# Storing the delta rule's solved blocks straight from where they are solved

## The chip, the cores and the metric

The kernel runs on one core of one Trainium2 chip. The metric is the device time of one execution in microseconds (us); lower is better. The engines are TensorE (PE, with its weight loads PEld), VectorE (DVE), ScalarE (ACT), GpSimd (POOL) and SyncE (SP), which issues nearly all transfers; a few are issued by ScalarE's own queue. 16 DMA engines carry the transfers.

## The reference, cut to what matters

The model has two layers over 512 latent tokens and 256 context tokens, width 1024: a bidirectional gated DeltaNet, then attention. The change lies in the DeltaNet layer, in the matrix that the chunked delta rule needs for each chunk of 64 tokens, each of 16 value heads and both directions:

```
a = jnp.where(strict, jnp.einsum('bhncd,bhnsd->bhncs', kb, kc) * decay, 0.0)
eye = jnp.eye(DN_CHUNK, dtype=F32)
t_inv = lax.linalg.triangular_solve(eye + a, jnp.broadcast_to(eye, a.shape),
                                    left_side=True, lower=True, unit_diagonal=True)
u = jnp.einsum('bhncs,bhnse->bhnce', t_inv, vb)
w = jnp.einsum('bhncs,bhnsd->bhncd', t_inv, kb * jnp.exp(gc)[..., None])
```

`t_inv` is a lower triangular 64x64 matrix per chunk, head and direction. Split in 32x32 blocks it has two solved blocks on the diagonal, one block beside it that is a product of the two and of the block of `a` between them, and one block that is zero. The recurrence reads it as the operand `cT`.

## The kernel before, in words

All is in fp32; the large products are split in a high and a low half (`wh`, `wl`, `uh`, `ul`) and made of three matmuls each. The first stage normalises the inputs and computes the modulation. The second, which the change touches (from about 100 to 602 us), projects the heads one after the other: eight key heads, eight query heads (`q_head`, numbered 0 to 7 here), then 16 value heads (`v_head`) and 16 gate heads (`z_head`) mixed. A head is 48 matmuls into PSUM tiles `g` (four buffers; a head uses two, so head n + 2 reuses those of head n), a convolution over tokens (L357 a copy by ScalarE, L360 four steps of VectorE per half) and a gate (L363 tanh by ScalarE, L372 for query heads and L365 for value heads by VectorE, into `sil_q`, `sil_v`). Its weights come three heads ahead: load L318 on SP, cast L319 on ScalarE, low half L320 on POOL or VectorE.

Between the heads run the pieces of the delta rule's matrices, for six tiles t of 128 rows (two chunks each) with 16 heads in the free dimension:
- `t_masked`: the keys' products are masked (`Gx`, L604, L605) and the decay between tokens is made. Its rows `df` are loaded on SP (L573), turned by ScalarE into exp(-|difference|) (L579, 16 activations of 128x64, then L580), and multiplied by VectorE (L560) into `md` (the diagonal blocks) and `mo` (the blocks beside it). L624 transposes `md` on VectorE into `L`, L625 scales it on POOL.
- `t_solve`: for two tiles at a time 31 steps of two instructions on POOL (L679, L680), from `L` to `X`.
- `t_join`: L695 turns `X` into `U0` and `U1` on VectorE, PE multiplies `mo` with one of them (`pp`), ScalarE negates it (`pn`, L707), PE multiplies again (`pw`, L713). ScalarE gathers the solved blocks from `U` (L705, eight copies of 32x512 a tile) and the products from PSUM (L716, four copies) in `Tt`, whose other blocks L555 has set to zero once on POOL, and L717 stores `Tt` to `t_d` in DRAM in one transfer of 1 MB. There are two `Tt`.
- `t_queries`: the decayed products of queries and keys (`df0q`, `df1q`, `qk_d`), on PE, VectorE, ScalarE and POOL.

`pieces` gives the order of these: the masks of tiles 0 and 1, then the solve of a pair woven with the masks of the next, then the joins of tiles 0 and 1 and the queries woven with the third solve, then the joins of tiles 2 to 5. After each head one to three pieces are written. That written order goes to a builder which orders each engine's instructions by its own estimates of their times; an engine then runs its instructions strictly in that order. Transfers on SP go out in its order too, each after the one eight before it has landed.

In the third stage, from 602 us, the recurrence reads `t_d` back as `cT` (L953); its first matmuls are L990.

Of the kernel before, what the change touches and what calls it, by code (L numbers as in the profile page):

```python
# [8 lines left out]
F32 = mybir.dt.float32  # L9
# [8 lines left out]
P = 128  # L18
# [4 lines left out]
NT = 6  # L23
QH, VH = 8, 16
# [73 lines left out]
def backbone(tc, a, out):  # L98
    nc = tc.nc
    V, S, G, T = nc.vector, nc.scalar, nc.gpsimd, nc.tensor  # L100
    dma = nc.sync.dma_start
# [8 lines left out]
    def dtile(shape, name):  # L110
        return dram.tile(shape, F32, tag=name, name=name)
# [15 lines left out]
    t_d = dtile([NT, P, 2, VH, 64], "t_d")  # L127
# [328 lines left out]
    for v in range(2):  # L456
        for d in range(2):
            c0 = ((v ^ d) * 2 + d) * 96
# [84 lines left out]

    tpool = tc.tile_pool(name="tpool", bufs=1, side="right", reuse_waits="tile")
    tp = tpool.__enter__()
    Tts = [tp.tile([P, 2, VH, 64], F32, tag=f"Tt{i}", name=f"Tt{i}") for i in range(2)]

    def of(b, d):

        return d ^ (b // 2)  # L550

    for Tt in Tts:
        for b in range(4):
            c0 = 32 - (b % 2) * 32
            G.memset(Tt[b * 32:b * 32 + 32, of(b, 1 - b % 2), :, c0:c0 + 32], 0.0)  # L555

    def decayed(E, o, dec, x):

# [128 lines left out]
    def t_join(t, st_):  # L687

        nm = f"_{t}"
        X, mo = st_[t - t % 2][1][:, t % 2], st_["mo", t]  # L690
        Tt = Tts[t % 2]

        U = [tp.tile([P, 2, VH, 32], F32, tag=f"U{d}", name=f"U{d}" + nm) for d in range(2)]
        for d, z_ in enumerate((X, X.rearrange("p i j -> p j i"))):
            V.transpose(U[d].rearrange("p v h j -> p j (v h)"), z_)  # L695
        yield
        pp = pa.tile([P, VH, 32], F32, tag="gq", name="pp" + nm)
        for h in range(VH):
            for b in range(4):
                i0, o0, d = b * 32, (b ^ 1) * 32, 1 - b % 2  # L700
                T.matmul(pp[o0:o0 + 32, h, :], mo[i0:i0 + 32, h, :], U[d][i0:i0 + 32, of(b, d), h, :], start=True, stop=True, tile_position=(i0, o0))
        for b in range(4):
            for d in range(2):
                r, c0 = slice(b * 32, b * 32 + 32), (b % 2) * 32
                S.copy(Tt[r, of(b, d), :, c0:c0 + 32], U[d][r, of(b, d)])  # L705
        pn = tp.tile([P, VH, 32], F32, tag="pn", name="pn" + nm)
        S.activation(pn, pp, AF.Copy, scale=-1.0)  # L707
        yield
        pw = pa.tile([P, VH, 32], F32, tag="gq", name="pw" + nm)
        for h in range(VH):  # L710
            for b in range(4):
                i0 = b * 32
                T.matmul(pw[i0:i0 + 32, h, :], U[1 - b % 2][i0:i0 + 32, of(b, b % 2), h, :], pn[i0:i0 + 32, h, :], start=True, stop=True, tile_position=(i0, i0))  # L713
        for b in range(4):
            c0 = 32 - (b % 2) * 32
            S.copy(Tt[b * 32:b * 32 + 32, of(b, b % 2), :, c0:c0 + 32], pw[b * 32:b * 32 + 32])  # L716
        dma(t_d[t], Tt)  # L717
        yield

    def side_by_side(*gens):  # L720
# [24 lines left out]
    def pieces():  # L745

        st_ = {}
        masked = lambda a, b: t_masked((a, b), st_)
        join = lambda a, b: one_by_one(t_join(a, st_), t_join(b, st_))
        queries = t_queries()  # L750
        yield from masked(0, 1)
        yield from weave(t_solve(0, st_), masked(2, 3), 2)
        yield from weave(t_solve(2, st_), masked(4, 5), 2)
        yield from weave(t_solve(4, st_), one_by_one(join(0, 1), queries), 3)
        yield from join(2, 3)
        yield from join(4, 5)
# [822 lines left out]
    po = pS.tile([P, 512], F32, tag="po", name="po1")  # L1579
# [49 lines left out]
    with tc.tile_pool(name="fo", bufs=2, side="right", reuse_waits="tile") as f2, tc.tile_pool(name="psO", bufs=1, space=PSUM, reuse_waits="tile") as pO:  # L1629
# [9 lines left out]
        for t in range(4):  # L1639
# [6 lines left out]
            for nh in range(2):  # L1646
                c = slice(nh * 512, nh * 512 + 512)
# [7 lines left out]
            r = ss[:, t, 0:1]  # L1655
# [3 lines left out]
            for hf in range(2):  # L1659
                c = t if hf == 0 else 7 - t  # L1660
# [35 lines left out]
```

## Time and profile before

| | us |
|---|---|
| three runs, median (lowest, highest) | 1264.22 (1263.83, 1269.48) |
| the profiled execution | 1262.34 |
| its span in the trace | 1260.6 |
| PE, DVE, ACT, POOL busy | 1155.4, 846.0, 714.9, 601.0 |

The span runs from the first to the last instruction that the profile shows; 1.7 us of the profiled execution's time lie outside it. Busy time of PE includes time at a lower granted clock. In the views, `out<-in` names the tiles an instruction writes and reads, `x48` is the count, and what stands in brackets behind a row of the timeline is the engine's idle time before it and what ended it.

### The profile page before, as it was taken

The numbers are of one execution on the slowest core, as the hardware profiler recorded it, in microseconds if no ns is written. First come the engines' busy times: TensorE is split into PE (matmuls) and PEld (weight loads), VectorE is DVE, ScalarE is ACT, GpSimd is POOL, SyncE is SP. The second block draws the span as 40 slices with busy tenths as digits, with TensorE's granted clock in tenths as the row PEclk, the third lists the DMA queues.
The fourth block names the chain that finished last, engine by engine and source line by source line (L and its number), as shares of the span: only waits on it lengthen the run. The fifth ranks groups of instructions, "written<-read, shape, count | busy, mean of one in ns | idle before, by whom it ended". The sixth has DMA issues, their size and how long they took to land.

```text
span 1260.6 us, 28128 instructions
## 1 busy us (share of the span) xinstructions
PE 1155.4 (92%) x10755; PEld 927.4 (74%) x10755; DVE 846.0 (67%) x1895; ACT 714.9 (57%) x1923; POOL 601.0 (48%) x486
## 2 busy tenths in 40 slices
PE   3999999999789979899999998989998989998996
PEld 1676778888677868788666665767776878888884
DVE  2688666868688556665688888577556756555535
ACT  3343436575575768973789886544443245665631
POOL 0131124149999999600585598257444043240540
PEclk9899999999899989899999999989999999999998
DMA  8465976556435588646979764655744021011133
GB/s 316 140 219 173 341 248 185 136 153 186 134 87 156 180 251 264 201 171 197 271 216 253 202 193 130 176 168 178 217 125 150 1 67 42 27 34 51 53 106 92
DMA packets 165495, 204.56 MB, mean 162 GB/s; under 512 B 13393, under 2 KB 114930, under 8 KB 164594
## 3 DMA queue, kind: packets, MB, share of 16 engines
q1 hardware_dynamic: 146546, 193.33, 50.2%
q10 hardware_dynamic: 18816, 9.44, 2.5%
q8 instruction: 85, 1.39, 0.5%
q14 instruction: 48, 0.39, 0.1%
HBM read 161.96 MB, written 40.67 MB: 161 GB/s over the span
## 4 chain that ended last, share of the span: by engine, by line
PE 51%; DVE 17%; ACT 10%; POOL 7%; DMA 7%; issue 6%; SPq 1%; ACTq 0%; DVEq 0%; POOLq 0%
PE ks L990 7%; PE g_z L338 6%; PE g_q L338 5%; PE g_k L338 3%; PE su L1045 3%; PE g_v L338 3%; PE pr L1015 2%; PE po L1515 2%; PE pg L1413 2%; POOL wol L874 2%; PE pso L1534 2%; PE kv L1296 2%; ACT pr L1479 2%; DVE acc_v L360 2%; POOL O L857 2%
## 5 line engine op out<-in xcount | busy, mean ns | idle before, releaser
L998 POOL TENSOR_TENSOR S<-S,glb 128x512 f32<-128x512 f32 x88 | 90.1, 1046 | 113.6 <-PE ks L990 113.4
L1130 PE MATMUL po<-woh,y 128*128 128x512 f32 x384 | 129.4, 405 | 1.0 <-DVE O L1048 0.8
L338 PE MATMUL g_v<-uh,wh 128*128 128x512 f32 (+1 forms) x256 | 90.1, 352 | 14.0 <-DVE sil_v L365 14.0
L680 POOL TENSOR_TENSOR X<-X,tmp 128x62 f32<-128x62 f32 (+15 forms) x93 | 96.7, 1040 | 6.5
L360 DVE SCALAR_TENSOR_TENSOR acc_v<-g_v,cwv,acc_v 128x510 f32<-128x510 f32 (+3 forms) x128 | 74.4, 608 | 33.5 <-ACT acc_v L357 31.9
L990 PE MATMUL ks<-S,ckq 128*64 128x256 f32 x768 | 93.5, 385 | 3.1 <-ACT o L995 2.5
L338 PE MATMUL g_z<-uh,wh 128*128 128x512 f32 (+1 forms) x256 | 89.2, 348 | 7.7 <-DVE sil_v L365 7.7
L679 POOL TENSOR_TENSOR tmp<-L,X 128x62 f32<-128x62 f32 (+15 forms) x93 | 89.1, 958 | 6.9
L338 PE MATMUL g_v<-ul,wh 128*128 128x512 f32 (+1 forms) x256 | 88.5, 346 | 0.0
L338 PE MATMUL g_v<-uh,wl 128*128 128x512 f32 (+1 forms) x256 | 87.9, 343 | 0.0
L338 PE MATMUL g_z<-uh,wl 128*128 128x512 f32 (+1 forms) x256 | 87.6, 342 | 0.0
L338 PE MATMUL g_z<-ul,wh 128*128 128x512 f32 (+1 forms) x256 | 87.6, 342 | 0.0
L874 POOL TENSOR_TENSOR wol<-wo,woh 128x512 fp32r<-128x512 f32 (+1 forms) x32 | 53.5, 1672 | 70.1 <-ACT woh L872 65.3
L1130 PEld LDWEIGHTS po<-woh,y 128*128 128x128 f32 x384 | 73.6, 192 | 16.8 <-DVE O L1048 1.2
L1130 PE MATMUL po<-wol,y 128*128 128x512 f32 x192 | 76.6, 399 | 7.6 <-POOL wol L874 7.6
L990 PEld LDWEIGHTS ks<-S,ckq 128*64 128x64 f32 x768 | 50.7, 136 | 42.1 <-ACT o L995 11.3
L320 POOL TENSOR_TENSOR wl_k<-w_k,wh_k 128x1024 fp32r<-128x1024 f32 x8 | 19.0, 2385 | 103.2 <-ACT wh_k L319 103.2
L338 PEld LDWEIGHTS g_v<-uh,wh 128*128 128x128 f32 x256 | 49.8, 194 | 20.6 <-DVE sil_v L365 14.7
L338 PEld LDWEIGHTS g_z<-uh,wh 128*128 128x128 f32 x256 | 49.2, 192 | 14.2 <-DVE sil_v L365 8.9
L1063 DVE TENSOR_TENSOR S<-su,S 128x512 f32<-128x512 f32 x88 | 56.5, 684 | 4.3 <-PE su L1045 3.1
L993 DVE SCALAR_TENSOR_TENSOR r<-ks,negV,cv 128x128 f32<-128x128 f32 x192 | 56.1, 344 | 4.1 <-PE ks L990 3.5
L1520 POOL TENSOR_TENSOR yT<-ay,yT 128x256 fp32r<-128x256 f32 x16 | 11.8, 738 | 97.4 <-ACT yT L1519 97.4
(409 smaller groups left out, 3400.8 us busy)
## 6 DMA issues: line engine op xcount, KB each, us to landing
aw<-in_ada_w SPq DMA_DIRECT2D x24, 1024.0 KB, 8.0
w<-in_dn_w_in SPq DMA_DIRECT2D x40, 512.0 KB, 4.4
wo<-in_dn_w_out SPq DMA_DIRECT2D x32, 512.0 KB, 3.7
cv<-v_d SPq DMA_DIRECT2D x80, 128.0 KB, 5.3
df<-gc_d SPq DMA_DIRECT2D x48, 128.0 KB, 2.8
z_d<-zs SPq DMA_DIRECT2D x16, 384.0 KB, 5.0
v_d<-vt ACTq DMA_DIRECT2D x16, 384.0 KB, 3.8
t_d<-Tt SPq DMA_DIRECT2D x6, 1024.0 KB, 5.0
```

What stands on the lines that cost most here:

```text
L338: mm = T.matmul(pg_[:m, :n], w[:, k, :m], u[:, k, c0:c0 + n], start=k == 0 and n_ == 0, stop=k == KT - 1 and n_ == 2)
L360: V.scalar_tensor_tensor(acc[:, c0 + lo:c0 + hi], ps[:, lo + j - 2:hi + j - 2], cwv[:, j, ct:ct + 1], acc[:, c0 + lo:c0 + hi], ALU.mult, A ...
L679: E.tensor_tensor(tv, bcast(L[:, :, j + 1:, j], 3, j + 1), bcast(X[:, :, j, 0:j + 1], 2, n), ALU.mult)
L680: E.tensor_tensor(X[:, :, j + 1:, 0:j + 1], X[:, :, j + 1:, 0:j + 1], tv, ALU.subtract)
L857: G.tensor_tensor(O[t][:, h], O[t][:, h], bcast(fo[:, t, h], 2, P), ALU.mult)
L874: G.tensor_tensor(wl[:, :c], w[:, :c], wh[:, :c], ALU.subtract)
L990: T.matmul(ks[r0:r0 + 64, w], kq[:, w, slot(hh), r0:r0 + 64], St[hh][:, d], start=True, stop=True)
L993: V.scalar_tensor_tensor(r[:, 2 * j + i], ks[:, 0, i], negV[:, visit, t, h0 + i:h0 + i + 1], v[:, 2 * hh + i], ALU.mult, ALU.add)
L998: G.tensor_tensor(St[hh], St[hh], bcast(g_, 3, P), ALU.mult)
L1045: T.matmul(su[c0:c0 + 64, d ^ j, j], kt[r0:r0 + 64, 4 * j + p, c0:c0 + 64], vd[r0:r0 + 64, 2 * j:2 * j + 2], start=True, stop=True)
L1063: V.tensor_tensor(St[hh], raw(sj, 0, [[512 - 1024 * j, 2], [P, 2], [1, P]]), St[hh], ALU.add)
L1130: T.matmul(acc[j][nh], y[i][:, j, :], ww[k][:, nh * 512:(nh + 1) * 512], start=h == 0 and x == 0, stop=h == VH - 1 and x == 2)
```

## The change

`Tt` and ScalarE's gathering go. One zero tile `none` of 128x2048 is set once, and six stores of 1 MB write it over all of `t_d` ahead of everything else. `keep` stores one block: 32 partitions, 16 heads, 32 numbers, that is 512 runs of 128 bytes, 64 KB. Eight `keep` a tile store the solved blocks from `U`, which gets two buffers; one ScalarE copy of the whole `pw` to `po_` takes the place of four, and four `keep` store the products from it. In the changed file lines behind the change are two or three higher, so L573 is L576 there, L579 is L582, L560 is L563, L624 is L627.

```diff
-    Tts = [tp.tile([P, 2, VH, 64], F32, tag=f"Tt{i}", name=f"Tt{i}") for i in range(2)]
...
-    for Tt in Tts:
-        for b in range(4):
-            c0 = 32 - (b % 2) * 32
-            G.memset(Tt[b * 32:b * 32 + 32, of(b, 1 - b % 2), :, c0:c0 + 32], 0.0)
+    none = tp.tile([P, 2, VH, 64], F32, tag="none", name="none")
+    G.memset(none, 0.0)
+    for t in range(NT):
+        dma(t_d[t], none)
+
+    def keep(t, b, d, c, tile_):
+
+        r = slice(b * 32, b * 32 + 32)
+        dma(t_d[t, r, of(b, d), :, c * 32:c * 32 + 32], tile_[r])
...
-        Tt = Tts[t % 2]
-
-        U = [tp.tile([P, 2, VH, 32], F32, tag=f"U{d}", name=f"U{d}" + nm) for d in range(2)]
+
+        U = [tp.tile([P, 2, VH, 32], F32, tag=f"U{d}", name=f"U{d}" + nm, bufs=2) for d in range(2)]
         for d, z_ in enumerate((X, X.rearrange("p i j -> p j i"))):
             V.transpose(U[d].rearrange("p v h j -> p j (v h)"), z_)
+            for b in range(4):
+                keep(t, b, d, b % 2, U[d][:, of(b, d)])
...
-        for b in range(4):
-            for d in range(2):
-                r, c0 = slice(b * 32, b * 32 + 32), (b % 2) * 32
-                S.copy(Tt[r, of(b, d), :, c0:c0 + 32], U[d][r, of(b, d)])
...
+        po_ = tp.tile([P, VH, 32], F32, tag="po", name="po" + nm)
+        S.copy(po_, pw)
         for b in range(4):
-            c0 = 32 - (b % 2) * 32
-            S.copy(Tt[b * 32:b * 32 + 32, of(b, b % 2), :, c0:c0 + 32], pw[b * 32:b * 32 + 32])
-        dma(t_d[t], Tt)
+            keep(t, b, b % 2, 1 - b % 2, po_)
```

The builder also orders other instructions anew. Numbers behind names are running numbers; those of the changed program are two lower for the same thing.

On SP, at the start of the tiles' pieces (`kk` are tile 0's keys, `df_0` its decay rows, `w` weights), before:

```order
L587 DMA kk_0_1883<-k_d 128x512
L587 DMA kk_0_1884<-k_d 128x512
L573 DMA df_0_1887<-gc_d 32x1024 x4
L573 DMA df_0_1892<-gc_d 32x1024 x4
L525 DMA q_d<-sil_q_1964 128x6x128
L318 DMA w_2265<-in_dn_w_in 128x8x128
```

and now:

```order
L590 DMA kk_0_1881<-k_d 128x512
L590 DMA kk_0_1882<-k_d 128x512
L576 DMA df_0_1885<-gc_d 32x1024 x2
L553 DMA t_d<-none 128x2048 x6
L576 DMA df_0_1885<-gc_d 32x1024 x2
L576 DMA df_0_1890<-gc_d 32x1024 x4
L525 DMA q_d<-sil_q_1962 128x6x128
L318 DMA w_2263<-in_dn_w_in 128x8x128
```

The six zero stores stand between the second and the third of tile 0's first decay loads, ahead of query head 1's store and the weights.

On ScalarE, where it turns these rows into decays (query heads 1, 2 and 3 have acc_q_1953, 2083, 2205 before and two lower now; L363 is a tanh), before:

```order
L357 ACTIVATE acc_q_1953<-g_q_1928,cwv 128x256
L363 ACTIVATE g_q_1928<-acc_q_1953 128x256
L579 ACTIVATE df_0_1887<-df_0_1887,gcV 128x64 x15
L489 ACTIVATE sq_q_1971<-sil_q_1964 128x768
L357 ACTIVATE acc_q_2083<-g_q_2033,cwv 128x512
L579 ACTIVATE df_0_1887<-df_0_1887,gcV 128x64
L319 CAST wh_2150<-w_2149 128x1024
```

and now:

```order
L363 ACTIVATE g_q_2153<-acc_q_2203 128x512
L582 ACTIVATE df_0_1885<-df_0_1885,gcV 128x64 x16
L363 ACTIVATE g_q_2178<-acc_q_2203 128x256
L582 ACTIVATE df_0_1890<-df_0_1890,gcV 128x64 x12
L583 ACTIVATE df_0_1885<-df_0_1885 128x1024
L582 ACTIVATE df_0_1890<-df_0_1890,gcV 128x64 x2
```

The first decay stood behind the tanh of head 1 and stands behind the first tanh of head 3; the second follows it at once.

On VectorE, around the gate of query head 4 (sil_q_2332 before, sil_q_2330 now; head 5 has acc_q_2415 and acc_q_2413), before:

```order
L360 SCALAR_TENSOR_TENSOR acc_q_2321<-g_q_2271,cwv,acc_q_2321 128x511
L372 SCALAR_TENSOR_TENSOR sil_q_2216<-g_q_2180,acc_q_2205 128x2x64 x2
L624 STREAM_TRANSPOSE L_2356<-md_2119 128x32x32
L360 SCALAR_TENSOR_TENSOR acc_q_2321<-g_q_2271,cwv,acc_q_2321 128x511
L360 SCALAR_TENSOR_TENSOR acc_q_2321<-g_q_2271,cwv,acc_q_2321 128x510
L360 SCALAR_TENSOR_TENSOR acc_q_2321<-g_q_2296,cwv,acc_q_2321 128x254
L360 SCALAR_TENSOR_TENSOR acc_q_2321<-g_q_2296,cwv,acc_q_2321 128x255
L372 SCALAR_TENSOR_TENSOR sil_q_2332<-g_q_2271,acc_q_2321 128x4x64 x2
```

and now:

```order
L360 SCALAR_TENSOR_TENSOR acc_q_2319<-g_q_2269,cwv,acc_q_2319 128x511
L563 TENSOR_TENSOR md_2117<-df_0_1890,Gx_1986 128x512
L563 TENSOR_TENSOR mo_2116<-df_0_1890,Gx_1986 32x512 x2
L360 SCALAR_TENSOR_TENSOR acc_q_2319<-g_q_2294,cwv,acc_q_2319 128x255
L360 SCALAR_TENSOR_TENSOR acc_q_2413<-g_q_2363,cwv,acc_q_2413 128x510
L360 SCALAR_TENSOR_TENSOR acc_q_2319<-g_q_2269,cwv,acc_q_2319 128x510
L627 STREAM_TRANSPOSE L_2354<-md_2117 128x32x32
L360 SCALAR_TENSOR_TENSOR acc_q_2413<-g_q_2388,cwv,acc_q_2413 128x254
L360 SCALAR_TENSOR_TENSOR acc_q_2319<-g_q_2294,cwv,acc_q_2319 128x254
L320 TENSOR_TENSOR wl_2489<-w_2487,wh_2488 128x1024
L360 SCALAR_TENSOR_TENSOR acc_q_2413<-g_q_2363,cwv,acc_q_2413 128x511
L372 SCALAR_TENSOR_TENSOR sil_q_2330<-g_q_2269,acc_q_2319 128x4x64 x2
```

Both products with tile 0's decays (the first pair stands five rows above this piece), the transpose, a weight's low half and three steps of head 5 now stand between the first steps and the gate of head 4; before, the products stood ahead of head 4's steps, and the low half and head 5 behind its gate.

## The prediction

> **What bounds the kernel now.** I read the table of busy time by stage first, because shares over the whole span mix a stage of projection matmuls with a stage of recurrence. The columns are the stretch, its length, and busy time of PE, PEld, DVE, ACT and POOL with their instruction counts, then the granted TensorE clock, the DMA share and GB/s.
>
> ```profile
> core 0: us, PE busy (x) PEld busy (x) DVE busy (x) ACT busy (x) POOL busy (x), PEclk, DMA share, GB/s
> 198.00:214.00 16.00, 16.00 (x173) 13.99 (x172) 8.64 (x19) 12.61 (x40) 2.39 (x1) 1.00 0.59 170
> 214.00:231.00 17.00, 17.00 (x137) 14.76 (x136) 15.34 (x28) 9.04 (x19) 6.92 (x3) 1.00 0.52 136
> 231.00:268.00 37.00, 37.00 (x325) 32.24 (x324) 28.97 (x51) 27.93 (x78) 0.09 (x1) 1.00 0.53 152
> 268.00:345.00 77.00, 69.56 (x642) 60.46 (x641) 55.37 (x65) 43.80 (x124) 71.71 (x66) 0.96 0.51 153
> 420.00:506.00 86.00, 73.89 (x545) 64.33 (x543) 46.65 (x77) 66.29 (x202) 81.93 (x68) 0.96 0.72 216
> 506.00:602.00 96.00, 93.57 (x1488) 81.32 (x1488) 59.39 (x90) 64.91 (x133) 19.62 (x17) 0.96 0.59 192
> ...
> 360.00:420.00 60.00, 55.10 (x824) 47.75 (x823) 50.34 (x61) 39.04 (x81) 54.91 (x48) 1.00 0.56 166
> 520.00:580.00 60.00, 58.52 (x1187) 50.57 (x1176) 42.12 (x56) 49.10 (x91) 9.55 (x4) 1.00 0.43 151
> ```
>
> From 198 to 268 PE never idles: whatever stops it there lengthens the program at once. From 268 POOL runs the triangular solves at 93 to 95% (71.71 of 77, 81.93 of 86), so POOL sets the pace there with PE close behind. The removed copies lie in the last two rows (360–420 and 520–580). ACT is busy there for 39.04 and 49.10 of 60 us; PE idles 60 − 55.10 = 4.9 us and 60 − 58.52 = 1.5 us. No more than those 6.4 us can come back by relieving ACT there. The waits of PE (who waited, for what: total, times, longest), in 268–345, 345–506 and 506–602, say where the rest of PE's idle time is:
>
> ```profile
> PE g_v L338 <- DVE sil_v L365: 7.2, 1, 7.2
> ...
> PE g_z L338 <- DVE sil_v L365: 6.9, 4, 3.7
> PE GQ0q L650 <- issue: 4.6, 1, 4.6
> ...
> PE g_v L338 <- DVE sil_v L365: 3.4, 1, 3.4
> ```
>
> These are waits for VectorE's half of a head. None names the copies L705 or L716.
>
> **The change part by part.** *Removed copies.*
>
> ```profile
> L705 ACT COPY Tt<-U 32x512 f32<-32x512 f32 x48 | 28.8, 617 | 2.5 <-DVE U L695 1.9
> L716 ACT COPY Tt<-pw 32x512 f32<-32x512 f32 x24 | 13.9, 578 | 2.7 <-PE pw L713 2.5
> L707 ACT ACTIVATE pn<-pp 128x512 f32<-128x512 f32 x6 | 3.6, 598 | 0.5 <-ACT vt L765 0.4
> ```
>
> ScalarE loses 28.8 + 13.9 = 42.7 us. It gains six copies of 128x512 from PSUM; the nearest row is L707, 598 ns each, so 3.6 us. Net −39.1 us of an engine with room in both stretches. Bounds of what that returns: nothing, if VectorE and POOL keep their pace; 6.4 us, if all of PE's idle there was ACT's doing. In 360–420 POOL is at 54.91 of 60 and leads into a stretch POOL sets, so I take nearly all of 520–580's 1.5 us and 1 us of the other: **−2.5 us**.
>
> *Added stores.* Per tile twelve stores of 64 KB in 128-byte runs (512 runs each) take the place of one store of 1 MB. Nothing before writes runs of 128 bytes, so I bound them. ScalarE's queue (q10) writes 512-byte runs:
>
> ```profile
> q10 hardware_dynamic: 18816, 9.44, 2.5%
> ...
> 117.30:117.60 0.30, 0.30 (x5) 0.30 (x4) 0.14 (x1) 0.30 (x1) 0.00 (x0) 1.00 0.68 131
> 480.00:500.00 20.00, 18.67 (x155) 15.76 (x154) 12.87 (x22) 15.52 (x45) 18.90 (x15) 1.00 0.93 272
> ...
> 508.00:511.00 3.00, 3.00 (x9) 2.32 (x8) 3.00 (x2) 3.00 (x10) 1.20 (x1) 0.50 0.88 309
> ```
>
> That is 2.5% of 16 × 1260.6 us over 18816 packets, 27 ns each. In 117.3–117.6 the queue writes the 256-byte runs of the cumulative gates: 131 GB/s × 0.3 us is 154 runs, in 0.68 × 16 × 0.3 us, 21 ns each. I take 21 ns for 128 bytes, since size has done little between these two; at the lowest it halves with the bytes, 10 ns. One store is then 32 runs on each of 16 engines, 0.67 us, and the 48 stores that fall in 520–580 (tiles 2 to 5) take 32 us. The room there is (1 − 0.43) × 60 = 34 us, plus four removed stores at 1.05 MB / (309/0.88 = 351 GB/s) = 3.0 us each, 46 us. They fit: **0 us**, and would still at 27 ns (41 us). Above 30 ns they don't, which is a rival below.
>
> The Trainium skill, page "DMA: Bandwidth & Descriptors", sections "Specifications" and "Measured", speaks against this change: it asks for runs of 512 bytes or more for full rate, says that shorter ones cost a read-modify-write, and calls transfers under 64 KB ruled by descriptors. By its 0.95 us for a 64 KB load (an estimate for this store) the 48 stores would take 46 us, just the room, and the sum would stay.
>
> On SP 72 issues replace 6. Rows: a store L717 issues in 0.32 us and a weight load in 0.38, so 66 × 0.35 = 23 us more of SP's time, most of it in 520–580, where weight loads stand behind the stores. The issues' row of these loads (the last number is us to landing), one load and its cast:
>
> ```profile
> w<-in_dn_w_in SPq DMA_DIRECT2D x40, 512.0 KB, 4.4
> ...
> 528.79 0.38 SPq L318 DMA_DIRECT2D w<-in_dn_w_in  x1
> ...
> 541.39 1.05 ACT L319 CAST wh<-w 128x1024 fp32r<-128x1024 f32 x1
> ```
>
> This leaves 541.4 − 528.8 − 4.4 = 8.2 us of cover. A tile's twelve issues are 4 us, so I cost it at **0**; without that cover it is up to 4 us a tile, 16 us.
>
> The end of the stage waits for nothing here:
>
> ```profile
> 576.70 0.32 SPq L717 DMA_DIRECT2D t_d<-Tt  x1
> ...
> 582.99 0.49 SPq L953 DMA_DIRECT2D cT<-t_d  x1
> ...
> L990 PE MATMUL ks<-S,ckq x768: 379/379/431, 602.0 to 780.2; 128*64 128x256 f32 x192
> ```
>
> The last block store goes out at 576.7, its reader's load at 583.0, the first recurrence matmul at 602.0: over 10 us of slack.
>
> *The zero fill.* Now six stores of 1 MB of zeros go out on SP after the second of the first decay loads (the rows of SP in the part on the change). In the run before, SP and ScalarE show:
>
> ```profile
> 194.93 5.07 SPq L573 DMA_DIRECT2D df<-gc_d  x8
> ...
> 200.38 3.70 ACT L579 ACTIVATE df<-df,gcV 128x64 f32<-128x64 f32 x15 [2.71 <-DMA df<-gc_d]
> 206.84 1.06 ACT L580 ACTIVATE df<-df 128x1024 f32<-128x1024 f32 x1
> 210.49 3.92 ACT L579 ACTIVATE df<-df,gcV 128x64 f32<-128x64 f32 x16
> ```
>
> The loads start at 194.93, 0.63 us each, so the fill begins near 196.5. It is 6.29 MB; at 351 GB/s that is 17.9 us, to 214.4. The remaining loads queue behind it: df0 of tile 0 is there at about 215.5 instead of 200.4. Here the written order matters: in the changed program ScalarE does this df after the tanh of query head 3 (before: of head 1), and on VectorE md and mo of tile 0, L's transpose and, new there, a weight split and steps of head 5 stand *ahead* of head 4's gate. Query head 6's projection reuses head 4's PSUM. VectorE before:
>
> ```profile
> 214.20 0.68 DVE L560 TENSOR_TENSOR md<-df,Gx 128x512 f32<-128x512 f32 x1
> 215.49 1.38 DVE L560 TENSOR_TENSOR mo<-df,Gx 32x512 f32<-32x512 f32 x2 [0.61 <-ACT Gx L605]
> ...
> 223.51 2.30 DVE L624 STREAM_TRANSPOSE L<-md 128x1024 f32<-128x1024 f32 x1
> 225.65 2.45 DVE L360 SCALAR_TENSOR_TENSOR acc_q<-g_q,cwv,acc_q 128x511 f32<-128x511 f32 x4
> 228.02 0.74 DVE L372 SCALAR_TENSOR_TENSOR sil_q<-g_q,acc_q 128x256 f32<-128x256 f32 x2
> ...
> 234.40 1.21 DVE L320 TENSOR_TENSOR wl<-w,wh 128x1024 fp32r<-128x1024 f32 x1
> ...
> 231.25 0.40 PE L338 MATMUL g_q<-uh,wh 128*128 128x512 f32 x1
> ```
>
> Before, head 4's gate was done at 228.76 and PE came to head 6 at 231.25 with no wait: 2.5 us of cover. After: df0 at 215.5, sixteen activations 3.92, then a tanh (0.4) and twelve activations of df1 (2.9), exp 1.06: 223.8. VectorE from there: md 0.68 + mo 1.38 = 2.06; head 4's five convolution steps at 0.6 or 0.5, 2.8, which first wait about 1.5 for ScalarE's copies of head 4; md and mo again 2.06; three steps 1.7; transpose 2.3; two steps 1.0; split 1.21; a step 0.6; the gate 0.74. Sum 2.06 + 2.8 + 1.5 + 2.06 + 1.7 + 2.3 + 1.0 + 1.21 + 0.6 + 0.74 = 16.0, so 239.8. PE waits 239.8 − 231.25 = **8.6 us** on a stretch without idle time. At the 272 GB/s and 0.93 share of 480–500 (292 GB/s) the fill takes 3.6 us longer, 12 us of wait; were the fill free, ScalarE's order alone (tanh of head 3 near 214.5, then df) keeps it near 7.5.
>
> *The clock after it.* What 3.42 us of idle did:
>
> ```profile
> 506.95 0.80 PE L338 MATMUL g_v<-uh,wh 128*128 128x512 f32 x1 [3.42 <-DVE sil_v L365]
> ...
> 513.20 0.39 PE L338 MATMUL g_v<-uh,wh 128*128 128x512 f32 x1
> ```
>
> Sixteen starts from 506.95 to 513.20, 15 steps in 6.25 us, against 0.23 a step at full clock (the next row starts at 513.43), 3.45: **+2.8 us**; the granted clock reads 0.50 there. Between 0 and 2.8.
>
> *Does the delay last?* POOL's solve starts when tile 1's L is there:
>
> ```profile
> 267.91 1.92 POOL L625 TENSOR_TENSOR L<-L,bball 128x1024 f32<-128x1024 f32 x1 [37.75 <-DVE L L624]
> ```
>
> It waits for VectorE, behind the same query heads, so solve and heads move together, and POOL's 93 to 95% leaves nothing to catch up with. The removed POOL memsets and the new one lie ahead of that 37.75 us wait and count for nothing.
>
> Sum: 1262.34 (the profiled execution) + 8.6 + 2.8 − 2.5 = 1271.2. The median of before stood 1.9 us over its profiled execution, so 1273.
>
> **The rivals.**
> *The stall is absorbed.* PE's 7.2 us wait near 330 and its 6.9 us on g_z are waits for VectorE too; if the heads arrive late, part of these waits goes. For it: they are as long as the stall. Against: they come from work behind POOL's solve, which starts late as well. Then 1262.3 + 11.4 − 7.2 − 2.5 + 1.9 = 1266. That is no change.
>
> *ScalarE's relief pays.* Place: PE's idle time in 360–420 and 520–580, 6.4 us, all of it returned because U, pn and pw follow each other sooner. It decides if head 4's gate is still done before 231, that is, if the decay loads overtake the fill and the order leaves head 4 alone. Then 1264.2 − 6.4 = 1258. Against: 360–420 is followed by a stretch set by POOL, and no wait names the copies.
>
> *Short runs bind.* From 30 ns a run the stores fill the room in 520–580. At 42 ns (twice my price) 48 × 32 × 42 ns = 64.5 us against 46, 18 late, less 8 of cover, +10: 1283. At 54 ns 83 us, +29: 1302. For it: only longer runs are priced. Against: 27 ns was paid for four times the bytes. By the Trainium skill's read-modify-write (same page and section "Specifications") a run would be moved twice, the 42 ns case; no run here shows it yet.
>
> *The numbers.* Forecast 0.58, its own range 1264.2 + 7.5 + 2.8 − 6.4 = 1268 to 1264.2 + 12 + 2.8 = 1279; absorbed 0.22; relief pays 0.10; short runs 0.10. Under 0.5% (±6.3 us, 1257.9 to 1270.5) a measurement of this kernel can't tell a difference. Of the forecast 0.08 lies below 1270.5. So faster 0.10 (the relief rival), same 0.22 + 0.08 = 0.30, slower 0.50 + 0.10 = 0.60. The range 1261 to 1286 leaves out the relief rival and the dearer half of the short runs, and some of the forecast's tails.
>
> **What would show it.** Right: the first df row of ScalarE at 215 or later with a wait for its DMA; a wait of PE of 7 to 12 us before a g_q at about 231, ended by DVE sil_q or ScalarE, with a granted clock near 0.5 behind it; POOL's L at 275 to 280; DMA share in 196–214 near 1. Wrong: PE without idle until 268 (then the fill or the order was misread), DMA share near 1 in 520–580 with weight casts waiting (short runs), or PE idle in 360–420 and 520–580 gone (relief).

## The result

The changed kernel takes 1280.15 us (median of six, 1276.52 to 1285.89), the kernel before 1266.06 on the same occasions (1263.83 to 1269.48). The ratio is 1.013 with a 95% interval of 1.0102 to 1.0159: slower, by 13 to 20 us. The forecast was 1273 with a range of 1261 to 1286. The changed kernel's profiled execution took 1276.52 us with a span of 1274.7; all comparisons of the two traces go by spans (1260.6 before), so 14.1 us are to be found.

The busy time by stage of the changed kernel, columns as in the prediction:

```profile
198.00:214.00 16.00, 16.00 (x191) 13.80 (x190) 9.56 (x20) 6.34 (x13) 3.98 (x4) 1.00 1.01 403
214.00:231.00 17.00, 17.00 (x117) 14.94 (x116) 8.81 (x18) 15.13 (x44) 3.81 (x2) 1.00 0.80 235
231.00:268.00 37.00, 26.86 (x233) 22.74 (x232) 27.34 (x46) 19.34 (x53) 2.87 (x2) 0.86 0.46 132
...
506.00:602.00 96.00, 88.14 (x1474) 76.31 (x1474) 64.73 (x88) 47.88 (x120) 33.65 (x28) 0.95 0.69 172
```

The DMA queues are full from 198 to 214 (share 1.01, 403 GB/s; it was 0.59). In 231–268, where PE had not idled at all, it now idles 10.1 us. ScalarE is relieved as meant: the row for 506–602 shows other work now, since the kernel runs late there, but in the last 100 us ahead of the recurrence (519–619) ScalarE is busy for 38.56 us, against 64.91 in 506–602 before. The place of the 10 us, on SP, ScalarE, VectorE, PE and POOL:

```profile
196.32 6.30 SPq L553 DMA_DIRECT2D t_d<-none  x6
202.66 7.99 SPq L576 DMA_DIRECT2D df<-gc_d  x6
213.05 0.38 SPq L525 DMA_DIRECT2D q_d<-sil_q  x1
...
214.71 0.59 ACT L363 ACTIVATE g_q<-acc_q 128x512 f32<-128x512 f32 x1
216.42 3.94 ACT L582 ACTIVATE df<-df,gcV 128x64 f32<-128x64 f32 x16 [1.12 <-DMA df<-gc_d]
223.45 1.04 ACT L583 ACTIVATE df<-df 128x1024 f32<-128x1024 f32 x1
...
224.52 0.69 DVE L563 TENSOR_TENSOR md<-df,Gx 128x512 f32<-128x512 f32 x1 [3.37 <-ACT df L583]
235.54 2.01 DVE L627 STREAM_TRANSPOSE L<-md 128x1024 f32<-128x1024 f32 x1
238.13 2.49 DVE L320 TENSOR_TENSOR wl<-w,wh 128x1024 fp32r<-128x1024 f32 x1
241.21 0.74 DVE L372 SCALAR_TENSOR_TENSOR sil_q<-g_q,acc_q 128x256 f32<-128x256 f32 x2
...
242.10 0.77 PE L338 MATMUL g_q<-uh,wh 128*128 128x512 f32 x1 [10.14 <-DVE sil_q L372]
...
237.63 1.91 POOL L628 TENSOR_TENSOR L<-L,bball 128x1024 f32<-128x1024 f32 x1 [5.67 <-DVE L L627]
281.38 1.92 POOL L628 TENSOR_TENSOR L<-L,bball 128x1024 f32<-128x1024 f32 x1 [41.83 <-DVE L L627]
```

The chain can be followed downwards: the fill goes out at 196.32, the decay rows behind it are there at 216.42, the first product with them starts at 224.52, head 4's gate ends at 241.95, and head 6 starts at 242.10 after 10.14 us of idle. POOL's solve starts 281.38 − 267.91 = 13.5 us later than before.

For the rest I took the start of the same matmul in both traces and subtracted. This is how late the changed kernel is at each place (start in the kernel before in brackets):

| first matmul of | later than before, us |
|---|---|
| query head 5 (221.91) | 0.6 |
| query head 6 (231.25) | 10.9 |
| gate head 0 (251.27) | 13.2 |
| gate head 4 (289.11) | 13.2 |
| value head 4, ahead of the joins (367.37) | 13.5 |
| value head 8, behind the joins of tiles 0 and 1 (432.23) | 12.5 |
| value head 11 (481.83) | 10.8 |
| tile 2's second product, pw (528.63) | 8.5 |
| gate head 11 (530.48) | 12.5 |
| value head 14 (541.31) | 19.6 |
| gate head 12 (565.69) | 16.9 |
| the recurrence, ks (601.96) | 17.0 |

So 12.7 us are lost at the fill and kept, some come back between 370 and 530, and 8.5 are lost a second time in the joins of tiles 3 to 5 and around them. The second loss was not in the prediction. PE's waits there, in the changed kernel from 537 to 619 (before, from 528 to 602, there were 0.9 and 0.6 us):

```profile
PE g_z L338 <- DVE sil_v L365: 3.0, 1, 3.0
PE pp L705 <- issue: 2.2, 1, 2.2
PE pp L705 <- DVE U L697: 0.9, 1, 0.9
PE pw L713 <- ACT pn L707: 0.6, 1, 0.6
```

The recurrence and all behind it took 1260.6 − 602.0 = 658.6 us before and 1274.7 − 618.9 = 655.8 after. The change touches nothing there, so some 3 us either way are the difference between two executions.

### The profile page after: what moved, and what is told of

Read it like the earlier page. It is cut to its first block, busy times and chain, and to the rows that moved or that the text cites. A ratio compares the mean times of both kernels' runs of the same rounds, so it can differ in the third digit from the quotient of the medians.

```text
span 1274.7 us, 28162 instructions
## 1 busy us (share of the span) xinstructions
PE 1155.7 (91%) x10755; PEld 928.4 (73%) x10755; DVE 849.8 (67%) x1895; ACT 677.5 (53%) x1857; POOL 599.5 (47%) x479
## 4 chain that ended last, share of the span: by engine, by line
PE 46%; DVE 16%; POOL 13%; DMA 10%; ACT 8%; issue 6%; SPq 1%; DVEq 0%; POOLq 0%; ACTq 0%
PE ks L990 7%; PE g_z L338 5%; POOL X L683 3%; POOL tmp L682 3%; PE po L1130 3%; PE g_k L338 3%; PE su L1045 3%; PE g_q L338 3%; PE pr L1015 2%; PE pg L1413 2%; PE pso L1534 2%; PE po L1515 2%; PE pg L1453 2%; PE pq L1037 1%; PE g_v L338 1%
## 5 line engine op out<-in xcount | busy, mean ns | idle before, releaser
L682 POOL TENSOR_TENSOR tmp<-L,X 128x62 f32<-128x62 f32 (+15 forms) x93 | 91.8, 987 | 6.6
L320 POOL TENSOR_TENSOR wl_k<-w_k,wh_k 128x1024 fp32r<-128x1024 f32 x8 | 19.0, 2385 | 103.7 <-ACT wh_k L319 103.7
L338 PEld LDWEIGHTS g_v<-uh,wh 128*128 128x128 f32 x256 | 50.3, 196 | 18.5 <-DVE sil_v L365 12.5
```

Of the source, the lines that this page charges most:

```text
L338: mm = T.matmul(pg_[:m, :n], w[:, k, :m], u[:, k, c0:c0 + n], start=k == 0 and n_ == 0, stop=k == KT - 1 and n_ == 2)
L682: E.tensor_tensor(tv, bcast(L[:, :, j + 1:, j], 3, j + 1), bcast(X[:, :, j, 0:j + 1], 2, n), ALU.mult)
```

## The experiments

Times are medians of repeated runs beside runs of the kernel before on the same chip (1263.5, 1264.3, 1263.9 and 1263.1 us in the four groups); ratios have 95% intervals.

**The fill alone.** The kernel before, with the fill at the change's place:

```diff
     for Tt in Tts:
-        for b in range(4):
-            ...
+        G.memset(Tt, 0.0)
+    for t in range(NT):
+        dma(t_d[t], Tts[t % 2])
```

> The kernel before with one addition: t_d is filled by six stores of 1 MB at the place where the change has them (from Tt, set to zero whole, so that no new tile is needed). ScalarE still gathers, and one store of 1 MB a tile still goes out. Fill theory: the loss of the change sits at the fill, so PE waits 8 to 11 us before query head 6 and the clock takes 2 to 3 us after it, +11 to +14 us over the kernel before, 1277 to 1280. Rival, that the stores in short runs or SP's longer queue lose the time in the join stages: this kernel has none of them and comes out within 5 us of before.

1276.69 us, ratio 1.0103 (1.0063 to 1.0143), +13 us. (SP sent three of the six stores behind the second decay load and three behind the third.) Its trace shows the same wait, in PE's waits from 180 to 300:

```profile
PE g_q L338 <- DVE sil_q L372: 9.4, 1, 9.4
```

Between query head 5 and gate head 0 it falls 14.92 − 3.17 = 11.7 us behind the kernel before, and nothing more after that (12.8 at the recurrence, 3.1 of which were there at query head 2 already). The fill accounts for the first loss by itself, with ScalarE's gathering and the long stores in place.

**The fill behind the decay loads.** Instead of between the second and third decay load of tile 0, behind all eight (six transfers later, since two of the eight went ahead of it already):

```diff
-    for t in range(NT):
-        dma(t_d[t], none)
...
+        for t in range(NT):
+            dma(t_d[t], none)
         yield from weave(t_solve(2, st_), masked(4, 5), 2)
```

(The builder sends it as soon as it can, so this line's effect on SP is that all eight loads go first; query head 1's store also goes out between the fill's second and third store.)

> The changed kernel with the six stores of zeros, still one after the other, eight transfers later on SP: behind the eight decay loads of tile 0 instead of between the second and the third. Fill theory in my form (the wait is for the decay rows queued behind the fill, and for the order written around them): PE does not wait before query head 6, the shift of 13 us there goes, and what stays is the loss in the joins of tiles 3 to 5, 1266 to 1271. If the 18 us of traffic do the harm themselves, wherever they stand (weights and tile 1's keys are queued behind them now), 1272 to 1280.

1267.16 us, ratio 1.0022 (1.0004 to 1.004). No wait of PE before head 6, POOL's solve near its old time, and the decay rows come early:

```profile
202.90 3.22 ACT L579 ACTIVATE df<-df,gcV 128x64 f32<-128x64 f32 x13 [3.92 <-DMA df<-gc_d]
...
269.93 1.92 POOL L625 TENSOR_TENSOR L<-L,bball 128x1024 f32<-128x1024 f32 x1 [38.74 <-DVE L L624]
```

The same 6.3 MB at nearly the same time cost 1 us at most here: the lag on the kernel before goes from 1.3 us at query head 2 to 2.3 at gate head 4. What was ahead of the decay rows cost 13 us. Whether the late rows or the order that the builder wrote around them weigh more is not told apart: both went together, and the kernel with the fill alone has both, too.

**The fill spread out.** One store behind each weight load of six heads:

```diff
+        if 8 <= n_ < 8 + NT:
+            with tc.issue_after(split_at[2]):
+                dma(t_d[n_ - 8], none)
```

> The changed kernel with the six stores of zeros moved: one behind each weight load of the first six gate heads, some 10 us apart, instead of six at once ahead of the first decay loads. Fill theory: PE does not idle before query head 6, POOL's first solve starts at 268 to 270 again, and the time is 1264 to 1269, near before. If the join stages lose time of themselves (the 8 us that PE lost against before between its second pw and the gate heads behind the joins), it stays 5 to 9 us above before, 1271 to 1275. Relief rival: 6 us below before, 1258 to 1261.

1269.24 us, ratio 1.0043 (1.0021 to 1.0064), at the upper edge of the fill theory's times and below those with a loss in the joins. The first loss is gone here too. What stays is the second: at value head 14 it is 7.7 us behind the kernel before, at gate head 11 only 1.35 and at the recurrence 4.7. The relief rival's 1258 to 1261 did not come.

**ScalarE's relief alone.** The kernel before without its 72 copies:

```diff
-                S.copy(Tt[r, of(b, d), :, c0:c0 + 32], U[d][r, of(b, d)])
+                pass
...
-            S.copy(Tt[b * 32:b * 32 + 32, of(b, b % 2), :, c0:c0 + 32], pw[b * 32:b * 32 + 32])
+            if b == 0:
+                S.copy(Tt[:, 0, :, 0:32], pw)
```

> The kernel before without ScalarE's gathering: the 48 copies from U and the 24 from PSUM are left out, and one copy of 128x512 a tile takes their place, as in the change; one store of 1 MB a tile stays, there is no fill and no short store. It leaves out placing the solved blocks, so the recurrence works on other numbers. Relief rival: PE's idle 6.4 us in the two join stages come back, 1258 to 1261. My term: 2.5 us, 1263 to 1264. If POOL and VectorE set the pace there: no change, 1265 to 1267.

1260.88 us, ratio 0.9974 (0.9952 to 0.9995): 2.6 us less by the medians, 0.6 to 6 by the interval. The time itself lies among those expected for the rival, because the kernel before took 1263.5 beside it; the difference is that of my term, 2.5, but the interval leaves out hardly more than the rival's full 6.4. In the trace this kernel goes from 0.2 us ahead of before at value head 4 to 2.2 at the recurrence, with ups and downs of 1 to 3 us between.

**Short stores with the gathering kept.** The kernel before, with its copies into `Tt`, but twelve short stores out of it, and the fill spread as above:

```diff
-        dma(t_d[t], Tt)
+        for b in range(4):
+            for d in range(2):
+                keep(t, b, of(b, d), b % 2, Tt)
+            keep(t, b, of(b, b % 2), 1 - b % 2, Tt)
```

> The kernel before with its gathering kept, but twelve stores of 64 KB in runs of 128 bytes out of Tt in place of one of 1 MB, and the zeros stored one by one as in the kernel with the spread fill. Against that kernel it differs by ScalarE's 39 us and by one pair of Tt instead of U and po_. If short runs and SP's issues cost nothing, as I took it, 1264 to 1268; if they are what the join stages lose, 5 to 9 us above before, and the same again in the kernel with the spread fill; if ScalarE's relief is worth 2.5 us, this kernel is 2 to 3 us slower than the one with the spread fill.

1264.66 us, ratio 1.0003 (0.9981 to 1.0024): no change. Short runs, 72 issues of SP and the spread fill together cost at most 3 us. But against the kernel with the spread fill and no gathering it is not 2 to 3 us slower, as the relief would have it, it is 4.6 faster. So something that only the direct stores bring with them costs more than the relief returns. Two things were left: `po_`, and the second buffer of `U`.

**One buffer of U.** The kernel with the spread fill, and one parameter:

```diff
-        U = [tp.tile([P, 2, VH, 32], F32, tag=f"U{d}", name=f"U{d}" + nm, bufs=2) for d in range(2)]
+        U = [tp.tile([P, 2, VH, 32], F32, tag=f"U{d}", name=f"U{d}" + nm) for d in range(2)]
```

> The changed kernel with the fill spread, as before, and U back to one buffer. Theory of the second buffer: it lets the next tile's transposes and pp be written ahead of the value heads, so that PE waits for VectorE between the joins of tiles 3, 4 and 5 (1.40, 0.48 and 1.72 us and a slower clock, 4 us in all in the run with the spread fill); with one buffer that goes, 1264 to 1266. Rival, that short stores and SP's queue lose it: the same 1268 to 1270 as with two buffers, or more, since the transposes now wait for stores to land.

1264.11 us, ratio 0.9997 (0.9978 to 1.0016), against 1.0043 with two buffers. Between gate head 11 and the recurrence it gains 1.1 us on before, where the one with two buffers lost 3.3. (Its profiled execution is 4.1 us behind from query head 2 on already, ahead of everything that the edits move: PE waits 1.4 us for a transfer of weights near 120, and the granted clock reads 0.67 in 130–140, where it reads 1.00 before.)

**One buffer, and the fill behind the decay loads.** The two edits shown above together.

> Both: the fill behind the eight decay loads, and one buffer of U. If the fill costs nothing there and the joins are as before, ScalarE's relief of 2 to 3 us is what remains: 1260 to 1264, no slower than the kernel before. If the traffic itself costs, 1268 or more.

1258.23 us, ratio 0.9949 (0.9932 to 0.9967): 6 us faster than the kernel before, the fastest version, and 2 us below what was expected. The fill costs nothing here: the lag on the kernel before is 0.7 us from query head 2 to value head 4. The version differs from the one with the fill behind the decay loads by U's buffers alone, and that one was at 1.0022: 9 us. Here the two traces show what the second buffer does. First the joins of tiles 3 and 4 on PE with two buffers:

```profile
535.72 1.15 PE L702 MATMUL pp<-U,mo 32*32 32x32 f32 x113
538.69 0.32 PE L702 MATMUL pp<-U,mo 32*32 32x32 f32 x15 [1.82 <-issue]
544.05 1.29 PE L710 MATMUL pw<-pn,U 32*32 32x32 f32 x128
545.19 0.98 PE L702 MATMUL pp<-U,mo 32*32 32x32 f32 x83
548.08 0.59 PE L702 MATMUL pp<-U,mo 32*32 32x32 f32 x45 [1.91 <-issue]
...
530.58 4.06 DVE L694 STREAM_TRANSPOSE U<-X 128x1024 f32<-128x1024 f32 x2
540.14 3.97 DVE L694 STREAM_TRANSPOSE U<-X 128x1024 f32<-128x1024 f32 x2
546.59 3.91 DVE L694 STREAM_TRANSPOSE U<-X 128x1024 f32<-128x1024 f32 x2
```

and with one:

```profile
534.83 1.27 PE L702 MATMUL pp<-U,mo 32*32 32x32 f32 x126
539.38 1.29 PE L710 MATMUL pw<-pn,U 32*32 32x32 f32 x128
547.27 1.29 PE L702 MATMUL pp<-U,mo 32*32 32x32 f32 x126
...
542.92 4.10 DVE L694 STREAM_TRANSPOSE U<-X 128x1024 f32<-128x1024 f32 x2
```

With two buffers tile 4's transposes need not wait until tile 3 has done with U. The builder then sets tile 4's pp right behind tile 3's pw and ahead of value head 14. PE, which runs in order, stands idle once in tile 3's pp (1.82 us) and once in tile 4's (1.91). It does not wait for U there: the transposes end at 534.64 and 544.11, ahead of the first matmul of either pp. The trace calls the wait "issue", so what released it isn't named. With one buffer tile 4's pp starts behind the first part of head 14, at 546.5, and PE does not stop in the pp of these two tiles.

**One buffer, and the fill over 290 to 400 us.** `fills = [13, 15, 18, 20, 21, 22]` in place of heads 8 to 13.

> One buffer of U, and the fill's six stores spread over 290 to 400 us, where the queues are half empty, each ahead of its tile's first block: 2 us were lost to the spread fill between 280 and 345. If they were lost to the fill's traffic among the loads there, this kernel gets them back, 1261 to 1264; if any store of 1 MB costs its share wherever it goes, 1264 to 1266.

1259.76 us, ratio 0.9963 (0.9947 to 0.9978): 4 to 5 us faster than before, a little below both expectations, and like the version above within the intervals. Two places for the fill do equally well; spread over some 240 to 300 us, among the decay loads of tiles 1 to 3 (0.9997), it takes most of the gain back. Which loads it holds up there is not shown.

**The change with one buffer of U.** The fill stays at its place.

> The changed kernel with one thing undone: U has one buffer again; the fill stays where the change put it. If the second buffer costs 5 to 7 us in the joins of tiles 3 to 5, whatever the fill does, this kernel is at +7 to +10 us over before, 1271 to 1275, with the wait of 10 us before query head 6 still there and none for VectorE's transposes at the joins. If the fill's late start and the second buffer are one loss seen twice, it stays at 1278 to 1281.

1275.71 us, ratio 1.0107 (1.0081 to 1.0134); the changed kernel was at 1.013. PE waits at the fill and nowhere for U:

```profile
PE g_q L338 <- DVE sil_q L372: 10.9, 1, 10.9
...
PE g_z L338 <- DVE sil_v L365: 3.0, 1, 3.0
PE pw L713 <- ACT pn L707: 1.1, 2, 1.0
```

It came out just above the 1271 to 1275 expected. Between gate head 11 and the recurrence it gains 0.9 us on before, where the change lost 4.5; the times differ by 2.9 us by the ratios, with intervals that overlap. The 3.0 us of gate head 11 stay in it: they are not the second buffer's, and the version with the fill behind the decay loads has no such wait.

**The second buffer without any short store.** The kernel without the gathering, with U in two buffers (and one `Tt` for the room):

> The kernel with ScalarE's gathering left out, no fill and one store of 1 MB a tile, and U in two buffers (one Tt instead of two, for the room). Like the kernel without the gathering it leaves out placing the solved blocks. If the second buffer's written order loses the time by itself, without any short store, this kernel is 4 to 7 us above the one with one buffer (which was at 0.9974 of before), so 1.001 to 1.003 of before, and PE waits 2 to 4 us at pp in the joins. If it needs the short stores, 0.997 again.

1263.63 us, ratio 1.0001 (0.9987 to 1.0015), against 0.9974 with one buffer: about 3 us, less than the 4 to 7 expected, and the two intervals overlap slightly. The same waits stand at pp:

```profile
PE pp L699 <- issue: 2.6, 2, 1.5
PE g_z L338 <- DVE sil_v L365: 1.3, 1, 1.3
PE pp L699 <- DVE U L693: 1.0, 1, 1.0
```

Its one-buffer fellow has none in that stretch. The loss comes with the buffer, not with the stores.

The traces of the four pairs agree better than their times. Between gate head 11 and the recurrence the version with two buffers falls behind its fellow by 5.4 us (the change itself), 4.8 (fill behind the decay loads), 4.4 (spread fill) and 4.8 (without short stores; this pair differs by a `Tt` as well). In all four with two buffers one tile's pw and the next tile's pp run back to back on PE; in no other trace do they.

What PE lacks in the pauses called "issue" is not settled, but the traces hold a hint. The profile has a queue that it calls "instruction" (q8), with 85 loads of 16 KB in every trace here. PE paused nine times for 0.9 to 2.2 us in the middle of a pp or pw, one of these in the kernel before; each time such a load ended 1.3 to 1.5 us before PE went on. PE's 21,510 matmuls and weight loads over 85 are 253 a load, and one pp, 128 of each, is through in 1.3 us. So PE may have run out of loaded instructions in a row of very short matmuls; no run tests this. Waits for U itself are 0.5 to 1.0 us, in three of the four.

## Why the prediction was right, and what it missed

*The wait at the fill: right.* The step said that the fill begins near 196.5, that df0 is there at 215.5, exp ends at 223.8, head 4's gate at 239.8, and PE waits 8.6 us; measured 196.32, 216.42, 224.5, 241.95 and 10.14. The working has the gate 2.2 us too early. It fell short by 0.7 us at the end of exp, by 1.3 for the second md, which took 2.01 us and not 0.68, and by 1.3 for the weight's split, which took 2.49 us and not 1.21; about 1 us of this came back in the other steps. POOL worked beside both (its L320 from 227.19 to 231.96, its L628, second last in the fence of the result, from 237.63 to 239.54), which I see only as a coincidence in time. The estimated 17.9 us for the fill held (403 GB/s in 198–214, not 351, but with the decay rows and head 1's store among it).

*The clock behind it: right in size.* PE right after the wait (timeline of the changed kernel):

```profile
243.09 0.63 PE L338 MATMUL g_q<-uh,wl 128*128 128x512 f32 x1
247.19 0.39 PE L338 MATMUL g_q<-uh,wh 128*128 128x512 f32 x1
```

and the stretch around it, with a granted clock of 0.64:

```profile
242.00:249.00 7.00, 6.90 (x20) 5.52 (x21) 3.98 (x11) 5.31 (x19) 0.00 (x0) 0.64 0.63 183
```

From 242.10 to 247.19 there are 12 steps in 5.09 us, against 12 × 0.23 = 2.76: 2.3 us, where the step said 2.8.

*That nothing absorbs it: right until 370, and nearly until 602.* The same 13.2 to 13.8 us stand from gate head 0 to value head 4, through the 7.2 us wait near 330 (now near 345), which is there unchanged: POOL's solve moved by 13.5 us with the heads. The absorption rival is refuted by that. From 370 to 528 up to 5 us came back; the kernel with the fill alone shows 15.1 at value head 8 and 12.7 at tile 2's pw, so about half of that comes without ScalarE's relief.

*ScalarE's relief: the term fits, but loosely.* 2.6 us alone by the medians, 0.6 to 6 by the interval. The rival's time of 1258 is out for the change as made, since its condition, head 4's gate before 231, did not hold. That the best version gains 6 us by timing, more than the relief alone, is not explained: by its trace it gains 1.5 + 0.7 = 2.2 us between query head 2 and the recurrence. (In the list of PE's waits the prediction takes every row for VectorE's half of a head; GQ0q, 4.6 us, is none, and no term rests on it.)

*Short runs: right that they don't bind, wrong in price.* In 568–569 hardly anything but block stores is in flight:

```profile
568.00:569.00 1.00, 1.00 (x10) 0.96 (x9) 0.04 (x1) 0.76 (x2) 0.00 (x0) 1.00 0.82 121
```

121 GB/s × 1 us are 945 runs in 0.82 × 16 us: 14 ns each, not 21. It is between the halved price of 10 and the 21 taken. The packets' own times in the trace say the same, a median of 13 ns. The kernel before has 1,024 packets of 128 bytes too, in its first 122 us, with a median of 11 ns, so a price could have been read there, though the trace doesn't say whether they are stores. That the stores in short runs cost at most 3 us shows also in the kernel that gathers and stores short. The rule of the Trainium skill ("DMA: Bandwidth & Descriptors", "Specifications") that runs under 512 bytes miss full rate holds: 121/0.82 = 148 GB/s of full queues here, against 403/1.01 = 399 for the fill. It does not decide the time, since the queues had room.

*SP's longer queue: 0, as taken, within those 3 us,* in the kernel that gathers and stores short, which has all of its issues.

*What the sum lacked: a term for U's second buffer.* The prediction costed the copies, stores, issues and the fill; the new `bufs=2` was in the diff and got no step. It belonged in the step on the removed copies, which took PE's idle time in 520–580 as something that could only shrink. The times put it at 3 us (without short stores; and in the change itself; in both the intervals overlap), 6 (spread fill) and 9 us (fill behind the decay loads), the traces at 4.4 to 5.4. The sum for the change is then 8.6 + 2.8 − 2.5 = 8.9, plus 1.5 and −0.5 for what the first two terms were short and long, plus 4.4 to 5.4: 14 to 15 us; measured 14 by the medians. Of the 7 us from the forecast of 1273 to 1280, 2 are the kernel before, which took 1266.06 on these occasions and not 1264.2; this term is the largest part of the other 5. The 1280 lies 1 us above the forecast's own 1268 to 1279. It is well inside 1261 to 1286 only because that range had room for short runs, which did not bind: so far it was luck, since the term that took the time up there was not in the sum.

## What to carry to other kernels

A block of bulk stores costs by what stands behind it on its queue: the same 6 MB cost 13 us ahead of six small loads and nothing behind them, so look at which loads feed the next chain and send those first. When a planner orders the engines, a second buffer is not only room: it lets work be set earlier, here one tile's small matmuls right behind another's, and on the engine that is the bound this cost some 5 us in all four pairs. So an added buffer needs a term, and its written order a look. Relief of an engine that isn't the bound returned little here: 39 us of copies removed gave 2.6 us by the medians, 6 at the most by the interval.

## What the runs showed of the hardware that was not expected

Stores in runs of 128 bytes took 14 ns a run per DMA engine, less than the 21 ns worked out for 256 bytes and the 27 ns for 512 in the kernel before, so the cost did fall with the size, if not in proportion. (Medians of the packets in the changed kernel's trace: 13 ns for 128 bytes, 18 for 256, 27 for 512, 46 for 1,024, 84 for 2,048.) In each of nine pauses of PE in rows of 32x32 matmuls a 16 KB load of the instruction queue had ended 1.3 to 1.5 us before PE went on. Six stores of 1 MB from one tile filled the queues to a share of 1.01 at 403 GB/s. And the stage from the recurrence on, whose instructions no version changes, took 655.6 to 663.4 us in the profiled executions (span less the first ks), so traces of two executions differ by up to 8 us there; the places of loss were read from the starts of matmuls ahead of it, and the sizes from repeated runs and from pairs of traces up to there.
